# Linear ReLU attention on one core: the gate ahead of nine stores reads the last K tile instead of the last V tile

## The chip, the cores and the metric

The kernel runs on one core of a Trainium2 chip. The metric is the device time of one execution in microseconds (us); lower is better. Times of one execution and the hardware profile of one execution are given. The profile's own clock starts at the first instruction (its "span"); the device time of the same execution is a little longer.

## What is computed

Q, K and V are float32 arrays of 8 x 12 x 512 x 64 (batch, heads, sequence, dimension). For each of the 96 heads:

```
Q_feat = np.maximum(0, Q)
K_feat = np.maximum(0, K)
KV = np.einsum('bhkd,bhkv->bhdv', K_feat, V)
K_sum = np.sum(K_feat, axis=2)
numerator = np.einsum('bhqd,bhdv->bhqv', Q_feat, KV)
denominator = np.einsum('bhqd,bhd->bhq', Q_feat, K_sum)
out = numerator / (denominator[:, :, :, None] + 1e-10)
```

Each of the three inputs is 12.58 MB, and so is the output: 37.75 MB are read from the chip's main memory (HBM) and 12.58 MB written.

## The kernel before

**Tiling.** The 96 heads are cut into `NG = 24` groups of four. A group's Q, K or V is 131,072 numbers (512 KB in float32), laid as 128 partitions of 16 rows of 64 numbers. Groups are numbered 0 to 23.

**Loads.** K and V of groups 0 and 1 come as float32 through the queues of SP and ACT (lines 85 to 89). All other loads are issued by POOL (GpSimd) and are cast to bf16 on the way (lines 76, 78 and 82): 512 KB read, 256 KB written into on-chip memory. POOL issues them all in program order, with its own waits for earlier loads and for buffers; the order at the end is written out by hand in lines 96 to 99: K22, V22, K23, V23, Q22, Q23. The last K load is thus followed by exactly three others: the last V load and two Q loads. The input pools hold 14 buffers each.

**Computation of a group.** DVE (VectorE) makes the masked ReLU of K and copies V (`prep`, lines 111 to 116). TensorE multiplies them (`mm_kv`, line 124), ACT moves the product out of PSUM (line 133), TensorE transposes Q (`transp`, line 139), ACT applies the ReLU (line 143), TensorE multiplies Q by the product (`mm_out`, line 154), and DVE divides by the denominator (`norm`, lines 165 to 168). The result is an `o_sb` tile of 512 KB in float32. The main loop (lines 188 to 201) is a software pipeline: in step g it runs `mm_kv(g)`, `prep(g+1)`, `mm_out(g-1)`, `norm(g-1)`, `store(g-1)` and then `transp(g)`.

**Stores and the gate.** `store` (lines 177 to 184) issues the output of a group on SP, as one DMA of 512 KB, and for groups 21, 22 and 23 as two halves. SP handles its instructions in order. Ahead of the store of group 15 (`NG - 2 - HELD`, with `HELD = 7`) stands one more DMA (line 179): it copies 64 numbers of the last V tile into a `scratch` tile that nobody reads. SP may issue it only once that tile has landed, so the stores of groups 15 to 23, nine groups in twelve DMAs, stay behind it in SP's queue until then. `outp` has `HELD + 4 = 11` buffers, which hold the finished outputs meanwhile. The order of every engine's work is the program's order (line 70).

Of the kernel before, what the change touches and what calls it, by code (L numbers as in the profile page):

```python
# [10 lines left out]
def kernel(  # L11
# [7 lines left out]
    nc = tc.nc  # L19
# [9 lines left out]
    NG = NH // NHG  # L29
# [38 lines left out]
    scratch = consts.tile([1, D], bf16, name="scratch")  # L68
# [3 lines left out]
    q_sb, k_sb, v_sb = {}, {}, {}  # L72
# [103 lines left out]

    def store(g, o_sb):
        if g == NG - 2 - HELD:
            nc.sync.dma_start(out=scratch, in_=v_sb[NG - 1][0:1, 0, :])
        parts = 2 if g >= NG - 3 else 1  # L180
        n = R // parts
        for j in range(parts):
            rs = slice(n * j, n * (j + 1))
            nc.sync.dma_start(out=Or[g].rearrange("p (r d) -> p r d", d=D)[:, rs], in_=o_sb[:, rs])
# [3 lines left out]
    for g in range(NG):  # L188
        mm_kv(g)
        evac_kv(g)  # L190
        if g + 1 < NG:
            if g + 1 < NB:
                zero(g + 1)
            prep(g + 1)
        if g > 0:
            mm_out(g - 1)
            store(g - 1, norm(g - 1))
        transp(g)
        evac_qt(g)
    mm_out(NG - 1)  # L200
    store(NG - 1, norm(NG - 1))


# [28 lines left out]
```

## Time and profile before

| quantity | before |
|---|---|
| median of 5 runs | 131.6 us |
| the five runs | 130.45, 131.39, 131.6, 131.71, 131.73 us |
| the profiled execution, device time | 131.71 us |
| its span | 129.9 us |
| busy in the span: PE, PE weight load, DVE, ACT, POOL | 59%, 44%, 62%, 39%, 31% |
| DMA queue of POOL (q0, casting loads) | 9792 packets, 17.83 MB written, 73.8% of 16 engines' span |
| DMA queue of SP (q1: stores, two first K loads, gate) | 4208 packets, 13.63 MB, 27.9% |
| instruction fetches (q8) | 13 packets, 0.21 MB, 0.6% |
| store of 512 KB, issue to landing | 6.7 us |
| casting load of K, issue to landing, median | 13.6 us |

A core's DMAs run on 16 DMA engines. The profile gives a queue's busy time as a share of what 16 engines have; because neighbouring packets overlap slightly, full engines show 1.0 to 1.1. The traffic figure counts written bytes, so a casting load appears with half of what it reads. "Landing" is the moment at which the semaphore of a DMA reports it complete.

### The profile page before, as it was taken

To read this page: it belongs to the slowest core of one execution; us is meant where nothing else is said; L and a number is where in the kernel's file an instruction comes from. 1 tells how busy PE (TensorE), PEld (TensorE's weight loads), DVE (VectorE), ACT (ScalarE), POOL (GpSimd) and SP (SyncE) were. 2 spreads that over 40 slices of the span, in tenths; PEclk is the share of its full clock that TensorE was granted. 3 is DMA by queue.
4 is the path that set the end of the run, shared out by engine and by line. 5 is a ranking of instruction groups with operands and counts; after the bars stand their busy time and mean duration, and the time that the engine had idled before them with its cause. 6 is when DMAs were issued, how large, how long until landed. Compare 5 with 4: busy or idle time off the path is not lost.

```text
span 129.9 us, 4118 instructions
## 1 busy us (share of the span) xinstructions
PE 76.9 (59%) x1728; PEld 57.3 (44%) x1728; DVE 80.5 (62%) x230; ACT 51.1 (39%) x121; POOL 39.7 (31%) x74
## 2 busy tenths in 40 slices
PE   0038847548557575585485575664857888686300
PEld 0037644426435444463364354452645565564200
DVE  1268856745847657558458477574587889597600
ACT  3025734533353345335433533443345366446000
POOL 6905333232523333315223233331234340000000
PEclk9999975555555555555555555555555555555555
DMA  4999999999999999999999999999999999979991
GB/s 116 375 292 209 212 192 276 269 229 284 238 258 283 229 270 263 235 283 256 238 289 236 259 281 235 264 274 230 281 208 208 216 206 209 190 240 401 397 386 69
DMA packets 14305, 32.76 MB, mean 252 GB/s; under 512 B 1616, under 2 KB 1616, under 8 KB 14288
## 3 DMA queue, kind: packets, MB, share of 16 engines
q0 software_dynamic: 9792, 17.83, 73.8%
q1 hardware_dynamic: 4208, 13.63, 27.9%
q10 hardware_dynamic: 288, 1.05, 2.1%
q8 instruction: 13, 0.21, 0.6%
q14 instruction: 4, 0.03, 0.1%
HBM read 37.75 MB, written 12.58 MB: 387 GB/s over the span
## 4 chain that ended last, share of the span: by engine, by line
DMA 78%; PE 5%; DVE 4%; POOL 3%; issue 3%; ACT 2%; POOLq 0%; ACTq 0%
DMA q_sb<-in_Q_dram 38%; DMA v_sb<-in_V_dram 30%; DMA k_sb<-in_K_dram 11%; PE ps_qt L139 2%; DVE o_sb L168 2%; PE ps_out L154 2%; ACT qt L143 2%; POOL q_sb L82 1%; PE ps_kv L124 1%; POOL k_sb L76 1%; POOL v_sb L78 1%; DVE vo L116 1%; DVE rec L167 1%; DVE den L165 0%; POOL ident masks.py:199 0%
## 5 line engine op out<-in xcount | busy, mean ns | idle before, releaser
L124 PE MATMUL ps_kv<-vo,kf 64*128 64x65 bf16 x768 | 25.2, 239 | 34.0 <-DVE vo L116 33.8
L133 ACT CAST kvd<-ps_kv 64x130 bf16<-64x130 f32 x96 | 25.4, 265 | 34.7 <-PE ps_kv L124 32.6
L124 PEld LDWEIGHTS <-kf 64*128 64x128 bf16 x768 | 21.5, 126 | 39.7 <-DVE vo L116 31.6
L143 ACT ACTIVATE qt<-ps_qt 128x1024 bf16<-128x1024 bf16 x24 | 24.6, 1024 | 32.7 <-PE ps_qt L139 32.7
L154 PE MATMUL ps_out<-kvd,qt 128*32 128x130 bf16 x768 | 29.0, 305 | 9.5 <-DVE o_sb L168 6.6
L168 DVE TENSOR_TENSOR o_sb<-ps_out,rec 128x512 f32<-128x512 f32 x48 | 33.2, 692 | 1.7
L114 DVE TENSOR_SCALAR kf<-k_sb,mask 128x1024 bf16<-128x1024 bf16 x44 | 19.4, 483 | 20.1 <-DMA k_sb<-in_K_dram 20.0
L154 PEld LDWEIGHTS <-qt 128*32 128x32 bf16 x768 | 17.6, 128 | 18.4 <-DVE o_sb L168 12.1
L82 POOL DMA_DIRECT2D q_sb<-in_Q_dram x24 | 15.5, 646 | 32.3 <-DMA k_sb<-in_K_dram 16.6
L139 PE MATMUL ps_qt<-ident,q_sb 128*128 128x128 bf16 x192 | 24.4, 307 | 1.0 <-DMA q_sb<-in_Q_dram 0.9
L139 PEld LDWEIGHTS <-q_sb 128*128 128x128 bf16 x192 | 18.2, 139 | 5.7 <-issue 4.2
L76 POOL DMA_DIRECT2D k_sb<-in_K_dram x22 | 12.0, 544 | 17.6 <-DMA v_sb<-in_V_dram 7.8
L78 POOL DMA_DIRECT2D v_sb<-in_V_dram x22 | 11.7, 533 | 16.9 <-DMA q_sb<-in_Q_dram 9.5
L116 DVE COPY vo<-v_sb 128x1024 bf16<-128x1024 bf16 x22 | 9.5, 430 | 11.5 <-DMA v_sb<-in_V_dram 11.5
L167 DVE RECIPROCAL rec<-den 128x8 f32<-128x8 f32 x48 | 9.8, 203 | 1.7
L165 DVE TENSOR_SCALAR den<-ps_out 128x8 f32<-128x8 f32 x48 | 7.6, 158 | 1.4 <-PE ps_out L154 1.4
L114 DVE TENSOR_SCALAR kf<-k_first,mask 128x1024 bf16<-128x1024 f32 x4 | 2.8, 750 | 5.2 <-DMA k_first<-in_K_dram 5.2
L133 ACT ACT_TABLE_LOAD x1 | 1.3, 1283 | 1.7 <-DVE kvd L107 1.7
L116 DVE CAST vo<-v_first 128x1024 bf16<-128x1024 f32 x2 | 1.4, 694 | 0.0
L105 DVE MEMSET mask<- 32x1 f32 x8 | 0.3, 59 | 0.9 <-PEq L216 0.8
L107 DVE MEMSET kvd<- 128x260 f32 x3 | 0.8, 275 | 0.0
masks.py:199 POOL TENSOR_SCALAR_AFFINE_SELECT ident<-ident 128x128 bf16<-128x128 bf16 x1 | 0.3, 289 | 0.1
(6 smaller groups left out, 0.8 us busy)
## 6 DMA issues: line engine op xcount, KB each, us to landing
out_dram<-o_sb SPq DMA_DIRECT2D x21, 512.0 KB, 6.7
q_sb<-in_Q_dram POOLq DMA_DIRECT2D x24, 256.0 KB, 12.4
k_sb<-in_K_dram POOLq DMA_DIRECT2D x22, 256.0 KB, 13.6
v_sb<-in_V_dram POOLq DMA_DIRECT2D x22, 256.0 KB, 13.5
out_dram<-o_sb SPq DMA_DIRECT2D x6, 256.0 KB, 4.3
v_first<-in_V_dram ACTq DMA_DIRECT2D x2, 512.0 KB, 6.7
k_first<-in_K_dram SPq DMA_DIRECT2D x2, 512.0 KB, 6.5
scratch<-v_sb SPq DMA_DIRECT2D x1, 0.1 KB, 2.7
```

Source lines behind the costliest of these rows:

```text
L76: nc.gpsimd.dma_start(out=k_sb[g].rearrange("p r d -> p (r d)"), in_=Kr[g])
L78: nc.gpsimd.dma_start(out=v_sb[g].rearrange("p r d -> p (r d)"), in_=Vr[g])
L82: nc.gpsimd.dma_start(out=q_sb[g].rearrange("p u f -> p (u f)"), in_=Qr[g])
L114: nc.vector.tensor_scalar(kf[g][:, :, s, :], k_sb[g], scalar1=0.0, scalar2=mask[:, s:s + 1], op0=Alu.max, op1=Alu.mult)
L116: nc.vector.tensor_copy(vo[g % NB][:, :, 0:D], v_sb[g])
L124: nc.tensor.matmul(ps_kv[g][:, t, 0:D1], kf[g][ts_, r, :, :].rearrange("p s d -> p (s d)"), vo[g % NB][ts_, r, :], start=(r == 0), stop=(r ...
L133: nc.scalar.copy(kvd[g % NB][64 * c:64 * c + 64, :, s, c, :], ps_kv[g][64 * s:64 * s + 64, :, 0:D1])
L139: nc.tensor.transpose(ps_qt[g][:, u, :], q_sb[g][:, u, :], ident)
L143: nc.scalar.activation(qt[g].rearrange("p u q -> p (u q)"), ps_qt[g].rearrange("p u q -> p (u q)"), Act.Relu)
L154: nc.tensor.matmul(po[hs, v // 2, (v % 2) * 2 * D1:(v % 2) * 2 * D1 + 2 * D1], qt[g][:, u, hs], kvd[g % NB][:, h // 2, h % 2, :, :], start ...
L167: nc.vector.reciprocal(rec, den)
L168: nc.vector.tensor_tensor(o_sb[:, 8 * j:8 * j + 8].rearrange("p (b r) d -> p b r d", b=2), pv[:, :, :, 0:D], rec.unsqueeze(3).to_broadcast ...
```

## The change

One word of the program: the gate DMA reads the last K tile in place of the last V tile. The number, order and sizes of all instructions on TensorE, DVE, ACT and POOL stay as they were; on SP the gate DMA keeps its place and its size of 64 numbers, and waits for another load.

```diff
     def store(g, o_sb):
         if g == NG - 2 - HELD:
-            nc.sync.dma_start(out=scratch, in_=v_sb[NG - 1][0:1, 0, :])
+            nc.sync.dma_start(out=scratch, in_=k_sb[NG - 1][0:1, 0, :])
         parts = 2 if g >= NG - 3 else 1
```

## The prediction

> **What bounds the kernel now.** I start with the slices and the chain of waits on the page, to see which resource is full.
>
> ```profile
> DMA  4999999999999999999999999999999999979991
> GB/s 116 375 292 209 212 192 276 269 229 284 238 258 283 229 270 263 235 283 256 238 289 236 259 281 235 264 274 230 281 208 208 216 206 209 190 240 401 397 386 69
> ...
> DMA 78%; PE 5%; DVE 4%; POOL 3%; issue 3%; ACT 2%; POOLq 0%; ACTq 0%
> ```
>
> The DMA engines are full in all slices but one near the end, and 78% of the chain is DMA; no compute engine is over 62% busy. So the bound is DMA work, and only an idle hole of these engines can be won. The GB/s line shows three phases: loads and stores mixed (about 260), loads alone (about 208, from 94 us), stores alone (about 395, from 116 us). The one slice below 9 lies between the last two phases. Next, the list of SP's waits, then the timeline at the gate:
>
> ```profile
> SPq L179 <- DMA v_sb<-in_V_dram: 25.8, 1, 25.8
> ```
>
> ```profile
> 113.54 0.61 SPq L179 DMA_DIRECT2D scratch<-v_sb  x1
> ...
> 114.25 10.06 SPq L184 DMA_DIRECT2D out_dram<-o_sb  x10
> ```
>
> SP waits 25.8 us for V23, opens at 113.54, spends 0.61 on the gate DMA and issues the first held store at 114.25. Now the same stretch by DMA (columns: engine busy times and counts, clock, DMA share, GB/s):
>
> ```profile
> 112.00:113.00 1.00, 0.86 (x32) 0.86 (x32) 0.93 (x4) 0.31 (x1) 0.00 (x0) 0.50 1.11 207
> 113.00:114.00 1.00, 0.83 (x24) 0.43 (x18) 0.93 (x4) 0.65 (x3) 0.00 (x0) 0.50 0.66 123
> 114.00:115.00 1.00, 0.74 (x18) 0.47 (x19) 1.00 (x4) 0.41 (x2) 0.00 (x0) 0.50 0.36 64
> 115.00:116.00 1.00, 1.00 (x14) 0.80 (x15) 0.93 (x4) 0.00 (x0) 0.00 (x0) 0.50 0.86 315
> ```
>
> Full is 1.11. From 113 us the share falls to 0.66 and 0.36, and climbs back within the fourth line: the trace's packet records have the first 4 KB store packet at 115.26 us. The hole is (1.11-0.66)/1.11 + (1.11-0.36)/1.11 = 0.41 + 0.68 us, and about 0.2 us more up to 115.26: some 1.3 us, as a mean over 16 engines. It is uneven. By the records of completion packets the earliest engines finish their last load at 112.8, the four latest at 115.10, 115.33, 115.46 and 115.74.
>
> The other end of the store phase, in the DMA view of 127.4 to 128.7 us (packets, MB, share of 16 engines):
>
> ```profile
> q1 hardware_dynamic: 17, 0.03, 6.1%
> ```
>
> 6.1% of 16 is one engine: fifteen are done by about 127.3, and one works alone until 128.68. The span ends 1.2 us later. Why that one? The view of 117.2 to 118.3 us has a visitor:
>
> ```profile
> q1 hardware_dynamic: 121, 0.43, 100.2%
> q8 instruction: 1, 0.02, 5.4%
> ```
>
> 5.4% of 16 engines over 1.1 us is one packet of 0.95 us, a 16 KB instruction fetch. In the packet records, store packets that otherwise take 0.16 to 0.17 us stretch to about 0.3 on one engine at 116.0 to 117.2. I read the fetch and the slowed packets beside it as the 1.5 us by which that engine ends late.
>
> **What the Trainium skill says.** "DMA: Bandwidth & Descriptors", section "Why a DMA increments its semaphore by 16 and not by 1": a DMA has landed only when every engine taking part has reported. The trace agrees: V23's last engine reports at 113.24, and the gate opens 0.30 us later. Section "Queues, rings and completion order": an engine goes round-robin between the queues it has work for, a whole packet at a time. The trace agrees: on the four late engines the tiny gate DMA, served at 114.8 to 114.95 by the others, waits for the end of the load in progress. One load's share per engine takes 1.25 us, so that looks like the turn. "Runtime: NRT & Kernel Launch", section "Instruction fetch mechanics": instructions come in 16 KiB blocks by a DMA queue; the 13 packets of q8 (0.21 MB) are that size.
>
> **The change part by part.** Nothing is added or removed; one wait ends earlier.
>
> 1. *How much earlier the gate opens.* K23 is issued on POOL at 102.52 and lands 9.7 us later, at 112.2; V23 at 103.78, landing 9.8 us later, at 113.54. Between loads of the loads-only phase, 256 KB at 209 GB/s is 1.25 us. So the gate opens 1.25 us earlier, at about 112.29. Bounds: 0.9 (jitter of receipts) to 1.35.
>
> 2. *SP's queue.* Behind the gate stand only the twelve stores. The gate's own issue (0.61) and the first store's 1.0 us from issue (114.25) to first byte (115.26) stay; the first byte moves to 114.0. SP is past store 14 since 87.65, so nothing else holds it. The outputs of groups 15 to 19 are long ready. POOL issued its last load at 106.31 and is passed by nothing.
>
> 3. *What the hole gives.* Engines that finished loading by 114.0 start storing 1.25 us earlier; those that finished at 114.5 gain about 0.8; the four late ones gain 0 to 0.2, having no hole. Total DMA work is unchanged. Mixing is not dearer: in the mixed phase a group takes 5.08 us (stores start every 5.08 us), against 3 x 1.25 + 1.29 = 5.04 in series.
>
> 4. *Who ends last then.* Ordinary engines: 127.2 - 1.25 = 125.95. The latest loader (115.74) needs six stores of 1.25 and six halves of 0.65, thus 115.76 + 11.4 = 127.15, as before. The engine with the fetch: its first store packet starts at 115.39, close to the common start and not with a late gate packet, so I take it as one of the twelve that had a hole; it ends at 128.68 - 1.25 = 127.43, or 127.9 if its hole was 0.8. That is the new end: 0.8 to 1.25 us earlier. I take 1.15.
>
> 5. *Is the last output ready?* The last half store was issued at 125.09 behind a backlog; it would now be due at 123.84. `norm(23)` ends at 122.45 + 0.69 = 123.14. Cover 0.7 us, if the last Q loads are not late. If one store is served ahead of a late Q load, that load slips by 1.29 us. Q23 (lands about 116.0, used at 118.09 by the transpose) has 2 us of room. Q22 is used on landing:
>
> ```profile
> 105.13 9.71 DMA q_sb<-in_Q_dram
> 114.84 0.05 issue
> 114.89 1.05 PE ps_qt L139 x8
> ```
>
> Its delay passes to `norm(23)`, which then ends at 124.4 at worst. On ordinary engines the last half's turn comes at 126.46 (before) - 1.25 = 125.2, and 124.4 plus 1.0 from issue to first byte is 125.4: 0.2 us late at worst, and nothing for the last engine, whose turn is 1.5 later. I cost this at nothing; the cover is the backlog.
>
> Sum: span 129.9 - 1.15 = 128.75. The profiled run took 131.71 with a span of 129.9, so 1.8 lie around it: 130.55. Its time stood 0.1 over the median of 131.6: 130.45, I say 130.5.
>
> **Rivals.**
>
> *B: the last engine had no hole.* If the fetch falls on an engine with its loads still running up to 115.1 or later (in this execution, or because it lands on another one in the next), filling the others' hole moves only engines that don't end last. For it: four of 16 engines have no hole, and the latest loader alone would end at 127.15. Against it: the start at 115.39. Time: 131.6, or 131.3 with a little luck.
>
> *C: slower, through Q22.* If the engines serve a backlog of stores before the loads, instead of in turn, the five to six stores ready at 114 delay Q22 on the late engines by up to 6 x 1.29 = 7.7 us; `norm(23)` then ends at 130.8. From its end to the span's end are at least 1.0 (issue to first byte) + 0.65 (half a store) + 1.2 = 2.85 us, so the span is 133.7, and the time 135.5. It decides once `norm(23)` ends after 129.9 - 2.85 = 127.05, a delay of 3.9 us, three stores ahead of Q22. For it: no stretch of the trace shows several stores queued behind each other while loads run. Against it: with one store queued the two share in turn (the store at 80.6 took 2.4 us from first to last packet over all engines, and a store alone 1.29), and three late engines were past Q22 at 114.0.
>
> *D: it does not do what it says.* If K23 and V23 landed together, nothing would move; 9.7 and 9.8 us after issues 1.26 us apart speak against it. Time 131.6; counted with B.
>
> **How the numbers follow.** A (hole filled for the last engine) 0.60, at 130.5, own range 130.1 to 130.9; B with D 0.28, at 131.3 to 131.6; C 0.12, from 132 to 135. About 1% (1.3 us) is what a measurement of this kernel can tell from no change. The five runs spread over 1.3 us, so each case carries about 0.4 on either side. A's largest gain, 1.25 us, is 0.95%: just below the bound, and noise carries it over in some four of ten. Faster by over 1%: 0.24; within: 0.65; slower: 0.11. The range takes A and B with their noise: 129.8 to 132.2.
>
> **What would show it.** Right: the gate's issue at about 112.3; first large store packets near 114.0; the DMA share at 113 to 115 us clearly above 0.66 and 0.36; Q22 still landing near 114.8 and `norm(23)` ending near 123.1; the last store packet near 127.4. B is right if all of that happens and one engine still ends at 128.7. C shows as Q22 landing past 117 and a DMA gap before the last halves. The forecast is wrong if the gate opens less than 0.8 us earlier, if the casting loads stretch on all engines once stores join, or if the fetch moves to an engine without a hole.

## The result and the profile after

The changed kernel is faster by half a per cent: 130.69 us median (43 runs, 130.34 to 131.34) against 131.52 us for the kernel before on the same chips (80 runs, 130.29 to 132.06). The ratio is 0.9947, with a 95% interval of 0.9937 to 0.9957; that is 0.57 to 0.83 us. The ratio and its interval are not the quotient of the two medians, which is 0.9937. The forecast was 130.5 us, within 1%, with a range of 129.8 to 132.2. Medians and ratios here and below leave out executions more than 1.5% above the fastest of the same kernel; there were four, all of them in e3.

One thing must be known before the trace is read. The profiled execution after took 131.34 us (span 129.6), the slowest of its 43. The two profiled executions therefore differ by 0.37 us only (131.71 to 131.34). A second trace of each kernel was taken among the experiments.

The slices and the chain on the page after:

```profile
DMA  3999999999999999999999999999999999989990
GB/s 121 381 290 208 211 190 273 284 219 278 237 259 278 232 271 266 231 286 249 247 287 234 261 276 233 274 262 233 287 209 210 210 209 210 199 291 402 408 383 28
...
DMA 81%; DVE 9%; issue 2%; POOL 2%; POOLq 0%
```

The dip between the loads-only and the stores-only phase is still there, at 8 tenths instead of 7; the slice in which stores take over moves 291 GB/s instead of 240. DMA remains the bound. SP's wait, and the timeline of SP at the gate:

```profile
SPq L179 <- DMA k_sb<-in_K_dram: 24.9, 1, 24.9
```

```profile
112.63 0.61 SPq L179 DMA_DIRECT2D scratch<-k_sb  x1
113.34 11.51 SPq L184 DMA_DIRECT2D out_dram<-o_sb  x12
```

The gate opens at 112.63 instead of 113.54: 0.91 us earlier, not 1.25. The steps behind it kept their lengths: 0.61 us of gate, the first store at 113.34, and by the packet records the first large store packet at 114.35 (before: 115.26), again 0.91 earlier. The same four microseconds as before, by DMA (last two columns: DMA share, GB/s):

```profile
112.00:113.00 1.00, 0.53 (x24) 0.26 (x16) 0.93 (x4) 0.74 (x3) 0.00 (x0) 1.00 1.10 205
113.00:114.00 1.00, 0.41 (x16) 0.23 (x16) 1.00 (x3) 0.32 (x2) 0.00 (x0) 1.00 0.67 123
114.00:115.00 1.00, 0.26 (x3) 0.26 (x4) 0.93 (x5) 0.00 (x0) 0.00 (x0) 0.58 0.84 250
115.00:116.00 1.00, 1.00 (x20) 0.81 (x19) 0.93 (x4) 0.13 (x1) 0.00 (x0) 0.50 1.07 402
```

The first half of the hole (0.67) is as it was; the second has gone from 0.36 to 0.84. With 1.11 as full, the missing part from 113 to 116 is (0.44 + 0.27 + 0.04) / 1.11 = 0.7 us; counted in the same way before it is (0.45 + 0.75 + 0.25) / 1.11 = 1.3. So about 0.6 us of idle DMA time is gone, near the measured gain.

At the end a lone engine works on, as before. The DMA view of 127.1 to 128.4 us, and that of 115.5 to 116.7:

```profile
q1 hardware_dynamic: 17, 0.03, 6.1%
```

```profile
q1 hardware_dynamic: 123, 0.45, 94.9%
q8 instruction: 1, 0.02, 5.0%
```

6.1% is again one engine of 16. By the completion packets, with which each engine reports its share of a DMA done, twelve engines end at about 126.3 (before: fifteen at 127.2), three at 126.9, and the last at 128.32 (before 128.68). The last instruction fetch is now at 115.64, still in the store phase, which here begins earlier. The engine that it falls on fares otherwise than before: by the packet records fifteen engines have started to store by 115.7, and the sixteenth sends its first store packet at 116.59, when the fetch is through.

### The profile page after: what moved, and what is told of

The parts are those of the page before. It is cut to its first block, busy times and chain, and to the rows that moved or that the text cites. A ratio compares the mean times of both kernels' runs of the same rounds, so it can differ in the third digit from the quotient of the medians.

```text
span 129.6 us, 4118 instructions
## 1 busy us (share of the span) xinstructions
PE 74.0 (57%) x1728; PEld 55.1 (43%) x1728; DVE 80.5 (62%) x230; ACT 51.1 (39%) x121; POOL 39.5 (31%) x74
## 4 chain that ended last, share of the span: by engine, by line
DMA 81%; DVE 9%; issue 2%; POOL 2%; POOLq 0%
DMA v_sb<-in_V_dram 49%; DMA q_sb<-in_Q_dram 18%; DMA k_sb<-in_K_dram 11%; DVE o_sb L168 5%; DMA out_dram<-o_sb 4%; DVE vo L116 2%; DVE rec L167 1%; POOL q_sb L82 1%; DVE den L165 1%; DVE kf L114 1%; POOL k_sb L76 0%; POOL v_sb L78 0%; POOL ident masks.py:199 0%; POOL ident masks.py:197 0%; POOLq masks.py:199 0%
## 5 line engine op out<-in xcount | busy, mean ns | idle before, releaser
L124 PE MATMUL ps_kv<-vo,kf 64*128 64x65 bf16 x768 | 24.3, 234 | 34.3 <-DVE vo L116 34.2
L124 PEld LDWEIGHTS <-kf 64*128 64x128 bf16 x768 | 20.7, 123 | 39.8 <-DVE vo L116 31.9
L154 PE MATMUL ps_out<-kvd,qt 128*32 128x130 bf16 x768 | 27.9, 294 | 10.8 <-DVE o_sb L168 6.8
L154 PEld LDWEIGHTS <-qt 128*32 128x32 bf16 x768 | 16.9, 124 | 19.5 <-DVE o_sb L168 12.1
L139 PE MATMUL ps_qt<-ident,q_sb 128*128 128x128 bf16 x192 | 23.6, 299 | 2.1 <-DMA q_sb<-in_Q_dram 2.1
L139 PEld LDWEIGHTS <-q_sb 128*128 128x128 bf16 x192 | 17.5, 135 | 6.5 <-issue 3.8
```

Of the source, the lines that this page charges most:

```text
L124: nc.tensor.matmul(ps_kv[g][:, t, 0:D1], kf[g][ts_, r, :, :].rearrange("p s d -> p (s d)"), vo[g % NB][ts_, r, :], start=(r == 0), stop=(r ...
L139: nc.tensor.transpose(ps_qt[g][:, u, :], q_sb[g][:, u, :], ident)
L154: nc.tensor.matmul(po[hs, v // 2, (v % 2) * 2 * D1:(v % 2) * 2 * D1 + 2 * D1], qt[g][:, u, hs], kvd[g % NB][:, h // 2, h % 2, :, :], start ...
```

## The experiments

Ratios are to the kernel before, on the same chip in the same session. Theory A: the gate opens so late that the DMA engines stand idle between the last loads and the first held store, and filling this hole is the gain. With it goes the claim that the engine hit by the last instruction fetch ends last. Theory B: the end is set by an engine that has no hole. Theory C: early stores make the last Q loads late. Theory F: the fetch has no part in the end.

**e1, the gate on the K load of group 22**, two loads ahead of the changed kernel's:

```diff
-            nc.sync.dma_start(out=scratch, in_=k_sb[NG - 1][0:1, 0, :])
+            nc.sync.dma_start(out=scratch, in_=k_sb[NG - 2][0:1, 0, :])
```

> Gate on the K load of group 22, two loads (2.5 us) ahead of the changed kernel's gate. Theory A (the gate's lateness leaves a hole in the DMA engines between the last loads and the first held store, and filling it is the whole gain): the gate opens near 110, the first large store packets come near 111.8, the DMA share never falls below 1.0 between 112 and 116 us, and the time is 0.9945 to 0.985 of before, at or below the changed kernel's 0.9947. Theory C (stores ahead of the last Q loads make norm(23) late and cost more than the hole): Q22 lands after 116, norm(23) ends after 125, ratio above 0.9947, and above 1.0 if three stores get ahead. If loads already taken in by an engine go first, Q22 lands at most one store (1.3 us) late.

Measured: 130.34 us, ratio 0.9908 (0.9891 to 0.9925). The gate opened at 109.94, but the packet records have the gate's first packet at 112.84 and the first large store packet at 112.86, a microsecond later than expected. The DMA share stayed at 1.02 or more from 112 to 117 us. Three of the engines finished their loads only at 116.8 to 117.5, so stores did get ahead of Q loads there: Q22's transpose began at 115.33 (after: 114.74). But `norm(23)` ended at 123.14, as in the kernel before. A is borne out. C's delay is real, 0.6 us at the transpose, and has cover.

**e5 and e11, the gate on the V load of group 22**, one load ahead of the changed kernel's (`in_=v_sb[NG - 2][0:1, 0, :]`), run twice:

> Gate on the V load of group 22: one load earlier than the changed kernel, one later than e1. Theory A (the gate's lateness leaves a hole, and the gain ends when the hole is closed): between the changed kernel (0.9947) and e1 (0.9908), so 0.990 to 0.995, with the first large store packets near 113.0 and little hole left. Theory C (stores displace the last Q loads): already worse than e1 only if Q22's delay reached the end, which e1 did not show; ratio above 0.995 would speak for it.

> The gate on V22 in more runs, as the fastest version so far: 0.9885 to 0.9930 of before. Theory A: no hole, DMA share above 1.0 in every microsecond from 112 to 117, engines ending between 125.4 and 127.3.

Measured: 130.25 us, 0.9909 (0.9876 to 0.9942), and in more runs 130.18 us, 0.9933 (0.9908 to 0.9959), just above its expected range (the quotient of its medians, 0.9903, lies inside). The windows of e5 show the hole closed:

```profile
113.00:114.00 1.00, 0.41 (x16) 0.23 (x16) 1.00 (x3) 0.30 (x2) 0.00 (x0) 1.00 1.08 289
114.00:115.00 1.00, 0.28 (x5) 0.28 (x6) 0.93 (x5) 0.00 (x0) 0.00 (x0) 1.00 1.07 342
115.00:116.00 1.00, 1.00 (x37) 0.90 (x36) 0.93 (x4) 0.56 (x1) 0.00 (x0) 0.70 1.04 397
```

In e11 the gate opened later, at 111.66 instead of 110.91, and the DMA share from 113 to 114 us was 0.96 where above 1.0 was expected. The gate on K22 gives no more than that on V22: although the gates of e1 and e5 opened 0.97 us apart, their first store packets came at the same time, 112.86 and 112.85, just after the first engine had finished its last load (112.81 and 112.79). So the gain ends where the hole is closed. What is left then is uneven work: the engines end between 124.7 and 127.2 us in e5, and between 125.3 and 127.2 in e11. This version is below both kernels of the study in its medians.

**e2, the gate on the Q load of group 22**, one load after the kernel before's (`in_=q_sb[NG - 2][0:1, 0, 0:D]`):

> Gate on the Q load of group 22, one load later than the kernel before. Theory A: the hole grows by 1.3 us on the engines that end last, ratio 1.006 to 1.011. Theory B (the end is set by an engine that loads until 115.7 and had no hole): the first store would come at 116.6 instead of 115.8 on that engine, ratio 1.003 to 1.007, and the gain of the changed kernel would have come from something else.

Measured: 131.73 us, ratio 1.0019 (1.0006 to 1.0033). That is under both expected ranges. The hole did grow, to about 2.5 us (windows of e2):

```profile
114.00:115.00 1.00, 0.18 (x9) 0.04 (x2) 0.93 (x5) 0.00 (x0) 0.00 (x0) 0.50 0.44 84
115.00:116.00 1.00, 1.00 (x12) 0.80 (x14) 0.93 (x4) 0.00 (x0) 0.00 (x0) 0.50 0.11 20
116.00:117.00 1.00, 0.99 (x32) 0.82 (x32) 0.66 (x1) 0.91 (x1) 0.00 (x0) 0.50 0.41 156
```

But no engine works alone at the end: all end at 128.5 to 128.7, while in the kernel before most end at 127.2 and one at 128.68. In this trace the last fetch lies at 114.46 us, inside the hole. Against the kernel before most engines lost 1.4 us and the last one nothing. That fits an end that no longer carries the fetch in its store phase; A's number for e2 had left the fetch where it was.

**e6, the gate on the very last load** (`in_=q_sb[NG - 1][0:1, 0, 0:D]`):

> Gate on the last load of all. Theory A with the fetch: in e2 all 16 engines already ended together, with the fetch inside the hole, so one more load of lateness has nothing left to hide in and costs its full 1.2 us against e2: ratio 1.009 to 1.013. If lateness of the gate costs nothing beyond e2's (another resource ends the kernel), ratio 1.001 to 1.005.

Measured: 133.02 us, ratio 1.0124 (1.0094 to 1.0154). The fetch was again in the hole (115.9), the engines ended together at 130.0 to 130.2, and one more load of lateness cost 1.3 us against e2. About 0.5 us of that is a slower first store, 1.02 us on SP instead of 0.51, so the ratio is in A's range with help that A did not foresee.

**e7, no gate at all** (line 179 and its condition left out):

> The gate DMA left out: the stores of groups 15 to 23 go as soon as their outputs are ready, among the loads. Theory A alone (only the hole counts) says as e1 or better, 0.985 to 0.991, as no hole is left. Theory C as the limit on the early side: the last loads are stretched from 1.25 us each to the mixed pace, Q23 lands 5 to 8 us later, norm(23) ends at 128 or later, and the last store follows it alone: ratio 1.005 to 1.025.

Measured: 134.50 us, ratio 1.0233 (1.0202 to 1.0263). The loads end at 122.4 instead of 115.7. The timeline of DVE has its last work at

```profile
128.79 0.69 DVE L168 TENSOR_TENSOR o_sb<-ps_out,rec 128x512 f32<-128x512 f32 x1
```

and the windows show the DMA engines starved meanwhile:

```profile
126.00:127.00 1.00, 0.14 (x12) 0.15 (x16) 0.57 (x1) 0.80 (x1) 0.00 (x0) 1.00 0.62 233
127.00:128.00 1.00, 0.49 (x32) 0.32 (x24) 0.61 (x3) 0.00 (x0) 0.00 (x0) 1.00 0.65 242
128.00:129.00 1.00, 0.00 (x0) 0.00 (x0) 0.93 (x4) 0.00 (x0) 0.00 (x0) 0.95 0.14 49
```

Here C decides: the hole has moved from 114 us to 128 us, where the last outputs are awaited. There is thus a best place for the gate, from V22 to K22 among those tried.

**e3, the kernel before with the fetch moved.** TensorE's program gets 40 more instructions at its start:

```diff
+    pad = pqt.tile([P, U, P], bf16, name="ps_qt")
+    for i in range(20):
+        nc.tensor.transpose(pad[:, i % U, :], ident, ident)
     zero(0)
     prep(0)
```

> The kernel before with 20 transposes of the identity matrix added at the start of TensorE's program, where TensorE is idle: 40 more instructions, so that each fetch [...] falls 40 instructions earlier. Theory A (one engine carries the last instruction fetch in the store phase and ends 1.5 us after the others, and so sets the end): the last fetch moves from 117.25 to about 115 or before, into or near the hole, the lone engine at the end loses up to 1 us of its lag, ratio 0.992 to 0.998. Theory F (the fetch does not set the end): ratio 0.998 to 1.002 and the lone tail at the end stays though the fetch has moved.

Measured: 130.91 us in the median of 18 runs, ratio 0.9967 (0.9942 to 0.9992). In the profiled execution (130.78 us) the last fetch of the main work was at 114.78, in the hole, and the view of 127.4 to 128.7 us, where the kernel before has one whole engine, has a quarter of one:

```profile
q1 hardware_dynamic: 9, 0.01, 1.8%
```

The last engine ended at 127.70, the others by 127.5. But the 18 runs spread from 130.27 to 132.02, and four more took 132.47 to 132.86. With these counted, the mean is 131.31 us against 131.44 for the kernel before, nearly no change. What the long ones did no trace shows. The one trace is as A says; the time doesn't settle it.

**e4, the same pad in the changed kernel:**

> The changed kernel with the same 20 transposes at the start. Theory A with the fetch as the last engine's burden: there the hole is nearly closed, so the fetch costs its 1 us wherever it lies unless it comes before 113; ratio 0.988 to 0.995 of before, and the distance to e3 shrinks to 0.2 to 0.8 us. Theory F: ratio as the changed kernel's, 0.993 to 0.9965, with the same distance to e3 as between the two kernels without the pad (0.8 us).

Measured: 130.72 us, ratio 0.9935 (0.9917 to 0.9953), inside both expected ranges. With the fetch at 115.81, in the store phase, the last engine ended at 127.55. The distance to e3 is 0.4 us by the ratios, in A's 0.2 to 0.8, but the two intervals together leave it uncertain by about as much, so F's 0.8 is not excluded. It tells nothing apart.

**e8, the kernel before with the fetch late in the store phase:** 60 small multiplications in place of the transposes, 120 instructions.

```diff
+    pad = pou.tile([P, 2, 512], fp32, name="ps_out")
+    for i in range(60):
+        nc.tensor.matmul(pad[:, 0, 0:16], ident, ident[:, 0:16], start=True, stop=True, skip_group_check=True)
```

> The kernel before with 60 small multiplications of the identity at the start of TensorE's program (120 instructions more), so that the last instruction fetch comes well inside the store phase, near 119 us, in every execution. Theory A (the engine with that fetch ends last): a lone engine ends 0.9 to 1.5 us after the others again, ratio 0.998 to 1.003, without runs near 130.3; e3, with the fetch near the hole, had a span of 129.0 in its profile. Theory F (the place of the fetch doesn't matter): no lone engine, or ratio as e3's, 0.994 to 0.999, with runs at 130.3 to 130.6.

Measured: 132.02 us, ratio 1.0050 (1.0029 to 1.0070), no run under 131.6. The fetch came at 122.2 (near 119 was expected), and the DMA view of 128.0 to 129.3 us has the lone engine again:

```profile
q1 hardware_dynamic: 17, 0.03, 6.1%
```

Most engines end at 127.7, one at 129.28: 1.5 us behind, as in the kernel before, and against F. The ratio is above both ranges. The first store took 1.14 us on SP instead of 0.52, and its first packet came at 115.77 instead of 115.26, which accounts for 0.5 us; why it took longer is open.

**e9, e10, second traces of the two kernels:**

> The kernel before once more, for a second trace. Theory A with the fetch: if the last fetch comes after 116 us, a lone engine ends about 1 to 1.5 us after the others and the time is near 131.5; if it comes before 115.3, in the hole, no lone engine and a time of 130.3 to 130.7. Theory F: no such link.

> The changed kernel once more, as its first profiled execution (131.34 us) was the slowest of its 43 runs. Expected of a typical one (130.7): the gate opens at 112.3 to 112.6, first large store packets at 114.1 to 114.4, ordinary engines end at 126.0 to 126.4, the last one at 127.4 to 127.9 instead of 128.3.

Measured: 131.57 us, ratio 1.0008 (0.9988 to 1.0029), and 130.58 us, ratio 0.9954 (0.9932 to 0.9976). The gate and the ordinary engines of e10 came slightly later than expected, its last engine at 127.90 as expected. The landmarks of both pairs (times from the traces, in us):

| | gate opens | first large store packet | most engines end | last engine ends | last fetch | device time of this execution |
|---|---|---|---|---|---|---|
| before | 113.54 | 115.26 | 127.2 | 128.68 | 117.25 | 131.71 |
| before, again | 113.73 | 115.45 | 127.4 | 128.66 | 117.11 | 131.66 |
| after | 112.63 | 114.35 | 126.3 | 128.32 | 115.64 | 131.34 |
| after, again | 112.71 | 114.44 | 126.7 | 127.90 | 114.50 | 130.93 |

The gate opens 0.97 us earlier in the mean of the pairs, and store packets and most engines follow by 1.0 and 0.8 us. Only the last engine moves less (0.4 and 0.8 us), and the device time goes with it (0.37 and 0.73).

**e12, one store fewer behind the gate** (`if g == NG - 1 - HELD:`, gate on K23):

> The changed kernel with the gate one store later in SP's queue: the store of group 15 goes among the loads, eight groups are held. Theory A: the loads end 1.3 us later, the stores have 1.3 us less to do, the hole is the same, so ratio 0.993 to 0.996, as the changed kernel. If the number of held stores mattered for itself (issue on SP, writes alone slower than mixed), the ratio would differ by more than 0.003 from 0.9947.

Measured: 130.70 us, ratio 0.9956 (0.9940 to 0.9972). As expected: holding eight groups instead of nine makes no difference that shows. The loads end later here (117.0 us) and the first store packet comes later (115.96); the hole, about 0.7 us by the windows of 114 to 117 us, is that of the changed kernel.

## Why the prediction was right, and where it was off

- *The bound and the mechanism* were right. The time follows the hole in order, though not in proportion: 0.9908 to 0.9933 where it is closed, 0.9947 where about 0.7 us remain, 1 where it is 1.3, 1.0019 where it is 2.5, 1.0124 with one load more.
- *Step 1, how much earlier the gate opens*, was sized too large: 1.25 us, measured 0.91 and 1.02. The 1.25 assumed that K23 takes as long from its issue to its landing in the changed kernel as in the trace before, 9.7 us. In the traces after it took 10.1 and 10.3, and in the second trace before 10.4; V23 took 9.8 and 10.1 before, 9.6 and 10.1 after. In these three the fetch before the last one lies at 110.6 us, as K23 comes in, and in the first trace before at 109.6. I suspect that it delays one of the 16 shares of K23. e2 goes with that (fetch at 110.96, K23 10.4, V23 9.7), e5 doesn't (110.88, both 9.5), and no run isolates it. The stated bounds (0.9 to 1.35) held.
- *Step 2* held: the issue of the gate, the first store and its first packet kept their distances.
- *Step 3* held in kind: mean idle time fell by 0.6 us, twelve engines ended 0.9 us earlier, and three of the late loaders gained only about 0.3 (126.9 against at most 127.3).
- *Step 4, who ends last*, was right that the engine with the fetch had a hole and would still end last. It was off in size, 127.43 forecast against 128.32 and 127.90, and in how that engine gains. The forecast let its whole store phase move up with the gate and kept the fetch inside it. In the two traces before, that engine stored first, from about 115.5, and met the fetch at 117.25 and 117.11. In both traces after, the fetch came ahead of its first store packet, at 115.64 and 114.50, and the store phase of this engine began only behind it, at 116.59 and 116.18. So its hole was not filled by stores, and it gained only 0.4 and 0.8 us. Its distance to most others was 1.5 and 1.3 us before, 2.0 and 1.2 after.
- *That the fetch makes the lone engine* agrees with the traces. The last engine is 1.2 to 2.0 us behind most others with the fetch in the store phase (117.25, 117.11, 115.64, 119.21 in e12, 122.2 in e8), and level with them with the fetch well ahead of the first store (114.78 in e3, 114.46 in e2, 115.9 in e6, where stores start at 118.2). The second trace after lies on the border: fetch at 114.50, first store at 114.44, still 1.2 us. In e4 and in the versions without a hole, engines end spread over 1.5 to 2.6 us anyway, and the fetch can't be told from the rest. No run removed the fetch, so its cost to the whole time is not shown by itself.
- *Step 5* held: `norm(23)` ended at 122.99 after and 123.14 before, and even the delays of e1 were covered.
- *The sum*: 1.15 us forecast, 0.70 measured (0.57 to 0.83). Both sizes, the gate's shift and the last engine's share of it, go that way. The forecast of "within 1%" stands.
- *Rivals B and D* fell: the gate moved, the time is below B's 131.3, and gating one load earlier still gained. A rival that the prediction did not name is that the gain comes from the fetch, which lies earlier in both traces after. It fails on the gates at K22 and V22: there the fetch lies at 117.24 to 118.62, as late as in the kernel before or later, and the times are the lowest. *Rival C* is not what this change does; e7 shows the mechanism at its price of some 3 us. One argument against C was miscounted: by the completion packets before, less 1.25 us, one late engine, not three, was past Q22 at 114.0.
- *The turn-taking* that I read into the waiting gate packets was too simple. In the trace after, the gate's packets were on the way from 113.88 (first engine served); the four late engines passed from Q22 to Q23 at 113.73, 114.20, 114.22 and 114.33, three of them later than that, but served the gate only after Q23, at 114.99 to 115.59. The prediction had read the Trainium skill ("DMA: Bandwidth & Descriptors", section "Queues, rings and completion order": an engine drains a whole packet of one queue, then turns to the next) with one load as the turn. These three engines took a further load first, so that reading does not hold there; the measurement decides. How long a turn is, no run shows. What the traces do show is in the last section.

## What to carry to other kernels

Where transfers of one kind are held back until those of another kind are through, compare the time from the release to the first byte (here 1.7 us) with the work still under way at the release: here a gate on the last V load left a hole of 1.3 us, one opening about 1 us earlier left half of it, and one opening 2.1 to 2.6 us earlier closed it or nearly so. Count the work engine by engine rather than by the mean share, since the last of 16 engines sets the end, and both a late load and an instruction fetch sit on single engines. Move such a gate one transfer at a time and stop where the gain stops: here a gate two loads ahead of the changed kernel's was as good as one load ahead, and no gate at all cost 2.3%.

## What the runs showed of the hardware that I had not expected

- A store issued while casting loads run starts late, as if it waited for loads that the DMA engines had already taken in; the traces show the delay, not its cause. In the kernel before, the store issued at 77.16 us has its first large packet at 80.62 and that of 82.24 at 85.69: 3.45 us, against 1.0 at 114.25, with most engines idle. The difference is about the time of two loads (2 x 1.25). In e1 the gate's first packet came 2.9 us after its issue, against 1.26 in the kernel before. So an earlier release is not paid at once by the loads next in line, and the place of the gate has some tolerance.
- The last 16 KB instruction fetch took 0.95 us in the kernel before (up to 1.70 in the second trace after), and in the kernel before four store packets of one engine took about 0.3 us each instead of 0.16 just ahead of it. The engine that ends last there is 1.3 to 1.5 us behind the others.
- In 64 runs of the kernel before in the last session, 11 were below 130.8 us and most lay at 131.3 to 131.9. A fetch that falls by chance into the hole would do this, but the low runs were not traced.
